# A hybrid decoder layer on one core: memory values computed by tokens, norm weights moved to ScalarE, first loads and landing estimates changed

## The chip, the cores and the metric

The kernel runs on 1 core of one Trainium2 chip. The metric is the device time of one execution in microseconds (us), median of several runs. The matmul engine is TensorE (PE in the profile; PEld is its weight load), the others are VectorE (DVE), ScalarE (ACT), GpSimd (POOL) and SyncE (SP); SP, ACT and POOL also issue DMA transfers.

## What is computed

One layer of a decoder, for 256 prompt tokens and 8 x 4 sampled tokens (288 columns in all), model width 2048, float32 throughout. Cut to what matters here:

```python
mkv = (rms_norm(mem_prompt, mem_norm_g) @ w_mem_kv).reshape(1, 256, 2, 4, 128)   # memory keys, values
h = rms_norm(x, norm_g)
c_h, c_b, c_c, c_g, q, n_g, b_g, kv6, m_q, m_g = split_cols(h @ w_in)            # 52 tiles of 128 columns
o_cmp, o_sel = nsa_cmp_sel(...)     # compressed and selected branches over a paged cache of 2048 tokens
o_win = window(...)                 # sliding window
o_m = gqa_attend(m_q, mkv keys, mkv values)                                       # memory attention
mixed = concatenate([y_conv, silu(n_g) * gated(o_cmp, o_sel, o_win), silu(m_g) * o_m])
y = rms_norm(x + mixed @ w_out, final_g)
```

The outputs are y, the new key and value rows, the window and convolution states, and the memory keys and values of the prompt (`mem_prompt_kv`).

## The kernel before

Activations lie transposed: 128 features on the partitions, tokens along the free dimension. A product of weights and activations is made in float32 precision from two parts of each operand: `wh` (the weights rounded, made by ScalarE) and `wl` (the rest, made by VectorE), and likewise `x_hl` and `m_hl`. For each 128 x 128 block three matmuls are added up: hi x hi, hi x lo, lo x hi. The weights come in **halves** `w0`, `w1`, ... of 128 x 1024 numbers, that is 8 blocks and 24 matmuls; two halves make one tile of 128 output columns. There are 152 halves: 16 of the memory weights (`w_mem`), 104 of `w_in`, 32 of `w_out`. A half is loaded into one of five buffers (`w_load`, six halves ahead), `w_hi(s + 2)` makes its `wh` two halves ahead into one of three buffers, `w_lo(s + 1)` its `wl` one half ahead into one of two. SP issues the loads up to half 13, POOL from half 14 on (`ON_SYNC`).

The order of all instructions is written by a planner in the same file, while the program is built: the main loop goes through the halves, and after every 12 matmuls `chunk()` advances a counter and lets each waiting generator (`spawn`) emit its next step. So an engine runs its instructions in exactly the order in which they were emitted, and waits where an operand is not ready. Times are guessed by a small cost table (`at[...]` for each engine); `until` and `behind` keep a generator back until an engine is thought to be done. The paged cache passes through 1024-wide staging buffers `st0` to `st5` (a seventh, in `qk1`, joins once the memory queries are used): `load_next` issues the next load as soon as a buffer is free, `loading()` estimates when it lands (`DMA_PIECE`, `DMA_LAG`), and `stage_stream` uses it when that estimate has passed. The uses are products of VectorE and GpSimd with `acmp` (`cmp_use`), scores (`sk`, `smd`) and values (`od`, `omd`) on TensorE.

The stages that the change touches, in order of time:

- Start: the first four halves multiply the memory tokens in plain float32 (`zf`), tile by tile as `memT` pieces (`mraw`, 16 planes of 128 x 256) and `w0` land; VectorE scales each piece by the norm's weights first (`mixed<-mraw`).
- Halves 4 to 15: the other six tiles of the memory weights, 256 columns wide (`proj(*m_hl, 256)`). Tiles 2 and 3 are keys. Tiles 4 to 7 are values: `mem_tile` multiplies the result by the row norm (`mvt<-z,Vc` on VectorE), a DMA writes it out, two TensorE transposes (`mvtp`) and two ScalarE copies bring it to the layout with tokens on the partitions.
- Meanwhile `prep_x` prepares x in six groups: sixteen VectorE instructions multiply by the norm's weight and the row norm (`rx<-rx,cst,rstd_x`), ScalarE and VectorE split each group into `x_hl`.
- Halves 16 to 119 (`w_in`, 288 columns), with the staged cache work and the attention of the prompt in between (`prompt_cmp`: `kcps`, `scp`, `scpt`; then `pct`, `acc`), and two passes over `w_out`.

Of the kernel before, what the change touches and what calls it, by code (L numbers as in the profile page):

```python
# [9 lines left out]
F32 = mybir.dt.float32  # L10
F32R = mybir.dt.float32r
I32 = mybir.dt.int32
AF = mybir.ActivationFunctionType
# [43 lines left out]
T_WIN = (20, 31)  # L57
T_LAST = 4
LAST_PASS = 272
DMA_PIECE, DMA_LAG = 1.75, 4.0  # L60
# [5 lines left out]
ON_SYNC = 14  # L66
# [11 lines left out]
def decode_step(ctx, tc, xT, xN, xD, memT, cst, w_in, w_mem, w_out, w_bg, pt, ptv, ckc, ckk, ckv, wk, wv, mk, mv,  # L78
                o_y, o_kv, o_mem, o_conv, o_wk, o_wv):
# [164 lines left out]
    def product_half(out, hi, lo, first, last):  # L244
        s = nhalf[0]
        nhalf[0] += 1
        w_hi(s + 2)
        w_lo(s + 1)
        wh, wl = his.pop(s), los.pop(s)
        mm = []  # L250
        for j in range(8):
            a = wh[:, j * 128:(j + 1) * 128]
            mm += [(j, a, hi(j)), (j + (0 if s > DIRECT + 1 else 4), a, lo(j)), (j + 8, wl[:, j * 128:(j + 1) * 128], hi(j))]
        mm.sort(key=lambda x: x[0])
        for n, (_, a, b) in enumerate(mm):
# [5 lines left out]
            matmul(out, a, b, start=(first and n == 0), stop=(last and n == 23))  # L261
            if n == 23 and LOW_FIRST <= s < NH - 18:
                w_lo(s + 2)
            if n % 12 == 11 and not (last and n == 23):
                chunk()
# [3 lines left out]
    def first_tiles():  # L269
# [3 lines left out]
        for k0 in (0, 8):  # L273
            for i in range(2):
# [23 lines left out]
                if k0 == 8:  # L298
                    yield z[i]

# [313 lines left out]
    def memk_use(j, t):  # L614
# [10 lines left out]
        if j == 1:  # L625
            spawn(mem_softmax(), 1)
        return
# [137 lines left out]
    rstd_m = Vc  # L765
    rstd_x = zt("C", "rstd_x")
# [23 lines left out]

    w_load(0)
# [6 lines left out]
    nc.sync.dma_start(raws[0][:, 512:], wsrc[0][:, 512:])  # L798
    m_load(4, 2, nc.scalar)
    m_load(6)  # L800
    nc.sync.dma_start(raws[1], wsrc[1])
# [68 lines left out]
    def mem_rstd():  # L870
        m_add(8)
        yield 1
        m_add(12)
        yield 1
        for n in (512, 256):
            vec.tensor_tensor(macc[:, :n], macc[:, :n], macc[:, n:2 * n], op=ALU.add)
        yield 3
        yield from token_rstd(rstd_m, [macc[:, 0:256]], 256, 1)
        env["rstd_m"] = True
        for i in range(8):  # L880
            while i not in mem_raw:
                yield 1
            dst = mem_raw[i]
            if i < 4:
                vec.tensor_tensor(dst, dst, rstd_m, op=ALU.mult)
            yield 1
            if i == 3:
                nc.gpsimd.dma_start(o_mem[0:4].rearrange("m p n -> p m n"), mkT)
            if i >= 4:
                nc.gpsimd.dma_start(o_mem[i], dst)  # L890
                yield 2
                t = ptr.tile([128, 512], F32, name=f"mvtp{i}", tag="t")
                for s in range(2):
                    transpose(t[:, s * 128:(s + 1) * 128], dst[:, s * 128:(s + 1) * 128], ident)
                for s in range(2):
                    act.activation(mvn(s, i - 4), t[:, s * 128:(s + 1) * 128], AF.Copy)
# [3 lines left out]
    def token_rstd(dst, planes, n, lag):  # L900
# [9 lines left out]
        r = small(3, "yr")  # L910
# [11 lines left out]
    def prep_x():  # L922

        g, r = C("ng"), rstd_x
# [17 lines left out]
    def sum_x():  # L942
# [25 lines left out]
        yield 2  # L968
# [39 lines left out]
    def mem_tile(i, z):  # L1008
        dst = mkT[:, i, :] if i < 4 else zt("A", "mvt")[:, :256]
        if i < 4:  # L1010
            act.activation(dst, z, AF.Copy)
        else:
            yield 2
            assert "rstd_m" in env
            vec.tensor_tensor(dst, z, rstd_m, op=ALU.mult)
        mem_raw[i] = dst
# [199 lines left out]
    def prompt_cmp():  # L1216
# [13 lines left out]
        act.activation(v, t[0:96, 128:384], AF.Copy)  # L1230
        vec.tensor_tensor(v[32:64], t[32:64, 128:384], v[32:64].bitcast(F32), op=ALU.subtract)
# [23 lines left out]
        yield 1  # L1255
        act.activation(pcv, pcv, AF.Exp, scale=SCALE)
        yield 1
        vec.tensor_reduce(sm, pcv, axis=AX.X, op=ALU.add)
# [93 lines left out]
    for i in range(2, 8):  # L1352
        then(mem_tile(i, proj(*m_hl, 256)))

# [195 lines left out]

def _inputs(x_prompt, x_sample, cache_kv, cache_win, state_conv, cache_mem, page_table, mem_prompt,
# [35 lines left out]
                w_mem=A(_ktiles(w_mem_kv[0])), w_out=A(_ktiles(wo)), w_bg=A(wbg), pt=A(pt), ptv=A(ptv), ckc=A(ckc), ckk=A(ckk), ckv=A(ckv),  # L1587
# [3 lines left out]
_OUTS = dict(o_y=(128, KT, NT), o_kv=(12, 128, NT), o_mem=(8, 128, 256), o_conv=(128, 72), o_wk=(4, 2, 128, 1024),  # L1591
# [3 lines left out]
def _outputs(r):  # L1595
# [10 lines left out]
            A(r["o_mem"].reshape(2, 4, 128, 256).transpose(3, 0, 1, 2))[None, None],  # L1606
# [16 lines left out]
```

## Time and profile before

| | us |
|---|---|
| runs | 620.51 median (618.64 to 622.23, 3 runs) |
| profiled execution, its own time | 619.23 |
| its span, first to last instruction | 616.4 |
| mean granted TensorE clock | 0.994 |
| VectorE, ScalarE, GpSimd busy | 458.6, 285.9, 200.4 |

The span is 2.8 us shorter than the execution's own time, and that execution lies 1.3 us below the median. The rows of the profile are read as engine, operation, output<-inputs, shapes, count | busy time in us, mean in ns of one | idle time of the engine before them, and what ended it.

### The profile page before, as it was taken

To read this page: it belongs to the slowest core of one execution; us is meant where nothing else is said; L and a number is where in the kernel's file an instruction comes from. 1 tells how busy PE (TensorE), PEld (TensorE's weight loads), DVE (VectorE), ACT (ScalarE), POOL (GpSimd) and SP (SyncE) were. 2 spreads that over 40 slices of the span, in tenths; PEclk is the share of its full clock that TensorE was granted. 3 is DMA by queue.
4 is the path that set the end of the run, shared out by engine and by line. 5 is a ranking of instruction groups with operands and counts; after the bars stand their busy time and mean duration, and the time that the engine had idled before them with its cause. 6 is when DMAs were issued, how large, how long until landed. Compare 5 with 4: busy or idle time off the path is not lost.

```text
span 616.4 us, 13330 instructions
## 1 busy us (share of the span) xinstructions
PE 600.2 (97%) x4893; PEld 557.9 (91%) x4893; DVE 458.6 (74%) x737; ACT 285.9 (46%) x500; POOL 200.4 (33%) x282
## 2 busy tenths in 40 slices
PE   8999999999999999999999999999999999999993
PEld 5998999989999899978998989888898898999993
DVE  5789899978477499988987879897568633357754
ACT  4855545544364345325434434353445444346650
POOL 2022545434234242323464523331212364122300
PEclk9999999999999999999999999999999999999997
DMA  8999898999888998897898998989898889677723
GB/s 313 407 403 402 261 328 314 319 312 368 310 287 303 362 388 309 295 385 267 295 316 260 318 366 288 297 283 332 303 355 321 337 285 312 225 253 276 234 86 153
DMA packets 74929, 188.40 MB, mean 306 GB/s; under 512 B 8752, under 2 KB 26064, under 8 KB 74608
## 3 DMA queue, kind: packets, MB, share of 16 engines
q0 software_dynamic: 26048, 100.48, 46.3%
q1 hardware_dynamic: 47664, 85.11, 39.0%
q10 hardware_dynamic: 1152, 1.97, 0.9%
q8 instruction: 38, 0.62, 0.4%
q14 instruction: 27, 0.22, 0.1%
HBM read 182.31 MB, written 13.60 MB: 318 GB/s over the span
## 4 chain that ended last, share of the span: by engine, by line
PE 82%; DVE 8%; DMA 6%; issue 2%; SPq 1%; ACTq 0%; ACT 0%; DVEq 0%
PE z L118 64%; PE od L118 3%; PE sk L118 3%; DMA st<-ckc 2%; PE zf L118 2%; DVE pooled L135 2%; DMA st<-ckk 2%; PE acc L118 2%; DVE wl L135 2%; PE s L118 2%; DMA qk<-ckk 1%; DMA mraw<-memT 1%; PE pt L123 1%; DVE st L135 1%; DVE ysum L135 1%
## 5 line engine op out<-in xcount | busy, mean ns | idle before, releaser
L118 PE MATMUL z<-x,wh 128*128 128x288 f32 x1664 | 254.5, 302 | 0.0
L135 DVE TENSOR_TENSOR wl<-w,wh 128x1024 fp32r<-128x1024 f32 x148 | 185.1, 1252 | 85.4 <-PE z L118 43.2
L118 PEld LDWEIGHTS z<-x,wh 128*128 128x128 f32 x1664 | 229.8, 188 | 7.8 <-issue 6.1
L135 ACT ACTIVATE wh<-w 128x1024 fp32r<-128x1024 f32 x148 | 154.4, 1052 | 19.1 <-PE z L118 14.5
L118 PE MATMUL z<-x,wl 128*128 128x288 f32 x832 | 127.0, 295 | 0.3 <-DVE wl L135 0.3
L118 PEld LDWEIGHTS z<-x,wl 128*128 128x128 f32 x832 | 115.8, 188 | 0.6 <-DVE wl L135 0.6
L350 POOL TENSOR_TENSOR st<-st,cst 128x512 f32<-128x512 f32 x63 | 69.3, 1102 | 131.5 <-DVE st L135 53.3
L219 POOL DMA_DIRECT2D w<-w_in x104 | 58.3, 560 | 109.3 <-DVE wl L135 79.2
L135 DVE TENSOR_REDUCE pooled<-st 128x16 f32<-128x1024 f32 x63 | 76.3, 1210 | 5.8 <-POOL st L350 5.8
L135 DVE TENSOR_TENSOR st<-st,cst 128x512 f32<-128x512 f32 x63 | 43.0, 684 | 10.6 <-DMA st<-ckc 10.5
L219 POOL DMA_DIRECT2D w<-w_out x32 | 17.5, 551 | 63.1 <-DVE wl L135 42.3
L578 POOL DMA_INDIRECT st<-ckv,rows_v x26 | 27.0, 1037 | 33.9 <-PE od L118 18.9
L118 PE MATMUL z<-y,wh 128*128 128x288 f32 x256 | 37.0, 297 | 0.0
L118 PE MATMUL z<-y1a,wh 128*128 128x288 f32 x224 | 35.4, 298 | 0.0
L118 PEld LDWEIGHTS z<-y,wh 128*128 128x128 f32 x256 | 35.1, 188 | 0.0
L118 PEld LDWEIGHTS z<-y1a,wh 128*128 128x128 f32 x224 | 31.4, 188 | 2.1 <-issue 1.2
L118 PE MATMUL z<-m,wh 128*128 128x256 f32 x192 | 27.3, 287 | 0.5 <-DVE mvt L135 0.5
L135 ACT ACTIVATE P<-P,nm 128x128 f32<-128x128 f32 (+1 forms) x32 | 14.2, 445 | 27.9 <-DVE nm L135 27.9
L118 PEld LDWEIGHTS z<-m,wh 128*128 128x128 f32 x192 | 24.7, 191 | 0.8 <-issue 0.7
L135 ACT ACTIVATE ysum<-z 128x288 f32<-128x288 f32 x16 | 6.6, 412 | 35.2 <-PE z L118 35.2
L118 PE MATMUL z<-y,wl 128*128 128x288 f32 x128 | 19.6, 295 | 0.0
L118 PE MATMUL sk<-st,qz 128*32 128x256 f32 x272 | 19.6, 383 | 0.0
(286 smaller groups left out, 691.6 us busy)
## 6 DMA issues: line engine op xcount, KB each, us to landing
w<-w_in POOLq DMA_DIRECT2D x104, 512.0 KB, 6.0
st<-ckc SPq DMA_DIRECT2D x126, 256.0 KB, 5.6
w<-w_out POOLq DMA_DIRECT2D x32, 512.0 KB, 5.1
st<-ckk SPq DMA_DIRECT2D x112, 128.0 KB, 4.6
w<-w_mem SPq DMA_DIRECT2D x13, 512.0 KB, 7.6
o_wk<-wk POOLq DMA_DIRECT2D x8, 512.0 KB, 6.1
o_wv<-wv POOLq DMA_DIRECT2D x8, 512.0 KB, 6.5
st<-mv SPq DMA_DIRECT2D x7, 512.0 KB, 6.5
```

Source lines behind the costliest of these rows:

```text
L118: nc.tensor.matmul(out, a, b, **kw)
L123: nc.tensor.transpose(out, a, b)
L135: return getattr(self.engine, name)(*args, **kw)
L219: (nc.gpsimd if s >= ON_SYNC else nc.sync).dma_start(raws[s], wsrc[s])
L350: done.append(eng.tensor_tensor(tm[:, :, kv], tm[:, :, kv], acmp[:, kv].unsqueeze(1).unsqueeze(1).to_broadcast([128, 2, 4, 64]), op=ALU.mu ...
L578: nc.gpsimd.indirect_dma_start(t, None, ckv, bass.IndirectOffsetOnAxis(ap=rows_v[:, j * 4 + b:j * 4 + b + 1], axis=0))
```

## The change

Five parts, in the order of the diff's weight:

1. **Memory values by tokens.** Halves 8 to 15 hold 2 blocks of 128 features by all 512 value columns (`_kpairs`). The memory tokens are now the stationary operand and the weights move: 12 matmuls of 512 columns for each half instead of 24 of 256. The result has tokens on its partitions, so ScalarE writes it with the row norm as scale (`mr`) straight to where the transposes put it; the output is written from there.
2. **Norm weights on ScalarE.** Sixteen ScalarE instructions scale x in place (`x_scales`), emitted one group for each half from half 6 on; VectorE then multiplies each group once by the row norm.
3. **First loads reordered.** Planes 4 and 5 of `memT` come from SP, planes 6 and 7 from ACT; the second part of `w0` and `w1` are cut in two.
4. **Estimates.** `DMA_LAG` 4.0 becomes 7.5 and, from chunk 165 on, 6.0; `DMA_PIECE` 1.75 becomes 1.6. Staging starts at chunk 22 (`STAGE_AT`), SP issues the loads up to half 18, the window's copies start later (`T_WIN`). Two waits between VectorE and ScalarE in `prompt_cmp` are counted (`behind`, `until`).
5. **An eighth staging buffer:** `qmz`, once the memory scores have used it.

```diff
-T_WIN = (20, 31)
+T_WIN = (33, 30)
-DMA_PIECE, DMA_LAG = 1.75, 4.0
+DMA_PIECE, DMA_LAG, LATER = 1.6, (7.5, 6.0), 165
+STAGE_AT = 22
-ON_SYNC = 14
+ON_SYNC = 19
...
-        return max(at[1], at[SYNC]) + DMA_LAG
+        return max(at[1], at[SYNC]) + DMA_LAG[now[0] >= LATER]
...
+    def run_half(s, mm, last, between=None):
+        m = len(mm) // 2
+        for n, (out, a, b, start, stop) in enumerate(mm):
...
-            if n == LOAD_AT:
+            if n == LOAD_AT * m // 12:
                 w_load(s + WR + 1)
                 next(x_next, None)
+                if s > 5:
+                    next(x_scale, None)
...
+    def mem_values():
+        z = [pz.tile([128, 512], F32, name=f"zv{tt}", tag="z") for tt in range(2)]
+        def out(tt):
+            planes = mixed[:, 12 + 2 * tt:14 + 2 * tt, 0:256]
+            act.activation(planes, z[tt].rearrange("p (a n) -> p a n", a=2), AF.Copy, scale=mr[:, tt:tt + 1])
+            nc.gpsimd.dma_start(o_memv[tt].rearrange("p (a n) -> p a n", a=2), planes)
+        for h in range(8):
...
+            for tt in range(2):
+                for k in range(2):
+                    hi, lo = (m_hl[n][:, 2 * h + k, tt * 128:(tt + 1) * 128] for n in range(2))
+                    w = slice(k * 512, (k + 1) * 512)
...
+                    mm += [(early, tt, hi, wh[:, w]), (early, tt, lo, wh[:, w]), (2.5 if h == 7 and not tt else 4, tt, hi, wl[:, w])]
...
         if j == 1:
             spawn(mem_softmax(), 1)
+            free.append(qmz.rearrange("p c b h n -> p (c b h n)"))
+            load_next()
...
+    def x_scales():
+        for i in range(6):
+            yield
+            k, t = xg[i]
+            for j in range(t.shape[1] // NT):
+                act.activation(xr[k + j], xr[k + j], AF.Copy, scale=C("ng")[:, k + j:k + j + 1])
...
-    nc.sync.dma_start(raws[0][:, 512:], wsrc[0][:, 512:])
-    m_load(4, 2, nc.scalar)
-    m_load(6)
-    nc.sync.dma_start(raws[1], wsrc[1])
+    m_load(4, 2)
+    nc.scalar.dma_start(raws[0][:, 512:768], wsrc[0][:, 512:768])
+    nc.sync.dma_start(raws[0][:, 768:], wsrc[0][:, 768:])
+    m_load(6, 2, nc.scalar)
+    for i in range(0, 1024, 512):
+        nc.sync.dma_start(raws[1][:, i:i + 512], wsrc[1][:, i:i + 512])
...
-                for j in range(k, k + n):
-                    vec.scalar_tensor_tensor(xr[j], xr[j], g[:, j:j + 1], r, op0=ALU.mult, op1=ALU.mult)
+                xv = x.rearrange("p (k n) -> p k n", n=NT)
+                vec.tensor_tensor(xv, xv, r.unsqueeze(1).to_broadcast([128, n, NT]), op=ALU.mult)
...
-        yield 1
+        yield from until(VEC, AHEAD)
+        behind(ACT, VEC)
         act.activation(pcv, pcv, AF.Exp, scale=SCALE)
         yield 1
+        behind(VEC, ACT)
         vec.tensor_reduce(sm, pcv, axis=AX.X, op=ALU.add)
...
-    for i in range(2, 8):
+    for i in range(2, 4):
         then(mem_tile(i, proj(*m_hl, 256)))
+    mem_values()
```

How the order moves, at the three places that the prediction leans on. First TensorE at half 8, the first of the values: before, 24 matmuls of 256 columns into `z` for each half; here the end of half 8 and the beginning of half 9.

```order
L118 MATMUL z_422<-m_110,wh_325 128x256
L118 MATMUL z_422<-m_111,wh_325 128x256
L118 MATMUL z_422<-m_110,wl_386 128x256 x8
L118 MATMUL z_422<-m_110,wh_384 128x256
L118 MATMUL z_422<-m_111,wh_384 128x256
```

After, the same place: 12 matmuls of 512 columns for each half, `zv` for the two groups of 128 tokens.

```order
L119 MATMUL ssq<-cst,mr 128x128 x2
L119 MATMUL zv_428<-wh_328,m_110 128x512
L119 MATMUL zv_428<-wh_328,m_111 128x512
L119 MATMUL zv_427<-wl_388,m_110 128x512 x2
L119 MATMUL zv_428<-wl_388,m_110 128x512 x2
L119 MATMUL zv_427<-wh_386,m_110 128x512
L119 MATMUL zv_427<-wh_386,m_111 128x512
```

The four `mvtp` pairs of transposes, which stood inside halves 12, 14, 16 and 18, are gone.

Second, ScalarE while the values are computed, before (each `wh` is one half of the weights, `x` a group's rounded part).

```order
L135 ACTIVATE wh_384<-w_257 128x1024
L135 ACTIVATE mixed<-z_324 128x256
L135 ACTIVATE rstd_x<-rx 128x288
L135 ACTIVATE wh_423<-w_281 128x1024
L135 ACTIVATE Vc<-ssq 128x256
L135 ACTIVATE x_112<-rx_247 128x864
L135 ACTIVATE wh_465<-w_316 128x1024
L135 ACTIVATE x_112<-rx 128x864
L135 ACTIVATE wh_512<-w_355 128x1024
```

And after, the same stretch with the groups' scaling.

```order
L136 ACTIVATE wh_386<-w_260 128x1024
L136 ACTIVATE rx_250<-rx_250,cst 128x288 x3
L136 ACTIVATE mixed<-z_327 128x256
L136 ACTIVATE rstd_x<-rx 128x288
L136 ACTIVATE wh_429<-w_284 128x1024
L136 ACTIVATE Vc<-ssq 128x256
L136 ACTIVATE rx<-rx,cst 128x288 x3
L136 ACTIVATE x_112<-rx_250 128x864
L136 ACTIVATE wh_460<-w_319 128x1024
L136 ACTIVATE x_112<-rx 128x864
L136 ACTIVATE rx<-rx,cst 128x288 x3
L136 ACTIVATE wh_486<-w_358 128x1024
```

Each group's three scalings now stand ahead of a `wh`, from half 10's on.

Third, SP's first loads, before, with what they wait for (DMAHW0 to DMAHW7 are the eight semaphores that the loads of SP and ACT take in turn).

```order
L798 DMA w_118<-w_mem 128x512
L770 DMA mraw_114<-memT 128x512
L801 DMA w_119<-w_mem 128x1024 [waits DMAHW0_49]
L770 DMA mraw_115<-memT 128x512 [waits DMAHW1_49]
L770 DMA mraw_115<-memT 128x512 [waits DMAHW2_49]
```

After:

```order
L815 DMA mraw_114<-memT 128x512
L854 DMA w_119<-w_mem 128x256
L857 DMA w_120<-w_mem 128x512 [waits DMAHW1_49]
L857 DMA w_120<-w_mem 128x512 [waits DMAHW2_49]
L815 DMA mraw_115<-memT 128x512 [waits DMAHW3_49]
L815 DMA mraw_115<-memT 128x512 [waits DMAHW4_49]
```

The ninth load, the first that waits for an earlier one to land, was `w1` on SP; it is now planes 6 and 7 of `memT` on ACT, and `w1` follows in two pieces.

More of the change, by code (lines that the diff above doesn't have):

```diff
@@ L254, in product_half @@
         mm.sort(key=lambda x: x[0])
-        for n, (_, a, b) in enumerate(mm):
+        run_half(s, [(out, a, b, first and n == 0, last and n == 23) for n, (_, a, b) in enumerate(mm)], last)
+    def run_half(s, mm, last, between=None):
+        m = len(mm) // 2
+        for n, (out, a, b, start, stop) in enumerate(mm):
             if s == DIRECT and n == 0:
                 w_load(s + WR)
-            if n == LOAD_AT:
+            if n == LOAD_AT * m // 12:
                 w_load(s + WR + 1)
                 next(x_next, None)
-            matmul(out, a, b, start=(first and n == 0), stop=(last and n == 23))
-            if n == 23 and LOW_FIRST <= s < NH - 18:
+                if s > 5:
+                    next(x_scale, None)
+            matmul(out, a, b, start=start, stop=stop)
+            if n == 2 * m - 1 and LOW_FIRST <= s < NH - 18:
                 w_lo(s + 2)
-            if n % 12 == 11 and not (last and n == 23):
+            if n == 7 and between:
+                between()
+            if n == m - 1:
+                chunk()
+            if n == 2 * m - 1 and not last:
                 chunk()
@@ L299, in first_tiles @@
                     yield z[i]
+    def mem_values():
[5 more added lines that the diff above has]
+        for h in range(8):
+            s = nhalf[0]
+            nhalf[0] += 1
+            w_hi(s + 2)
+            w_lo(s + 1)
+            wh, wl = his.pop(s), los.pop(s)
+            mm = []
+            for tt in range(2):
+                for k in range(2):
+                    hi, lo = (m_hl[n][:, 2 * h + k, tt * 128:(tt + 1) * 128] for n in range(2))
+                    w = slice(k * 512, (k + 1) * 512)
+                    early = 2 * tt + (k if h == 7 and tt else 0)
+                    mm += [(early, tt, hi, wh[:, w]), (early, tt, lo, wh[:, w]), (2.5 if h == 7 and not tt else 4, tt, hi, wl[:, w])]
+            mm.sort(key=lambda x: x[0])
+            i = [[n for n, x in enumerate(mm) if x[1] == tt] for tt in range(2)]
+            run_half(s, [(z[tt], a, b, h == 0 and n == i[tt][0], h == 7 and n == i[tt][-1]) for n, (_, tt, a, b) in enumerate(mm)],
+                     h == 7, (lambda: out(0)) if h == 7 else None)
+        assert "rstd_m" in env
+        out(1)
+        chunk()
     def proj(hi, lo, N):
@@ L765, in decode_step @@
     rstd_m = Vc
+    mr = one.tile([128, 2], F32, name="mr")
     rstd_x = zt("C", "rstd_x")
@@ L877, in mem_rstd, with token_rstd @@
         yield 3
-        yield from token_rstd(rstd_m, [macc[:, 0:256]], 256, 1)
+        yield from token_rstd(rstd_m, [macc[:, 0:256]], 256, 1, mr)
         env["rstd_m"] = True
-        for i in range(8):
+        for i in range(4):
             while i not in mem_raw:
                 yield 1
-            dst = mem_raw[i]
-            if i < 4:
-                vec.tensor_tensor(dst, dst, rstd_m, op=ALU.mult)
+            vec.tensor_tensor(mem_raw[i], mem_raw[i], rstd_m, op=ALU.mult)
             yield 1
[L887 to L896, printed above, removed]
+        nc.gpsimd.dma_start(o_mem.rearrange("m p n -> p m n"), mkT)
     GROUPS = ((0, 0), (128, 0), (160, 96))
-    def token_rstd(dst, planes, n, lag):
+    def token_rstd(dst, planes, n, lag, r):
         groups = [x for x in GROUPS if x[0] + 128 <= n]
@@ L967, in sum_x @@
         nc.sync.dma_start(wbg, w_bg)
-        yield 2
+        while now[0] < STAGE_AT:
+            yield 1
         for t in buffers:
@@ L1008, in mem_tile @@
     def mem_tile(i, z):
[L1009 to L1016, printed above, removed]
+        act.activation(mkT[:, i, :], z, AF.Copy)
+        mem_raw[i] = mkT[:, i, :]
+        return
+        yield
     cos, sin = C("cos"), C("sin")
@@ L1254, in prompt_cmp @@
         vec.tensor_tensor(pcv, pcv, bc(mx), op=ALU.subtract)
-        yield 1
+        yield from until(VEC, AHEAD)
+        behind(ACT, VEC)
         act.activation(pcv, pcv, AF.Exp, scale=SCALE)
         yield 1
+        behind(VEC, ACT)
         vec.tensor_reduce(sm, pcv, axis=AX.X, op=ALU.add)
```

14 lines of the change are left out of this document (8 added, 6 removed).

## The prediction

> **What bounds the kernel now.** I read the page first, then TensorE's waits, then the windows of the early stage.
>
> ```profile
> span 616.4 us, 13330 instructions
> PE 600.2 (97%) x4893; PEld 557.9 (91%) x4893; DVE 458.6 (74%) x737; ACT 285.9 (46%) x500; POOL 200.4 (33%) x282
> PE 82%; DVE 8%; DMA 6%; issue 2%; SPq 1%; ACTq 0%; ACT 0%; DVEq 0%
> ```
>
> TensorE is busy for 97% of the span and carries 82% of the chain that ended last. A busy row alone could hide stalls, so the second view is what TensorE waited for in all.
>
> ```profile
> PE zf L118 <- DVE mixed L135: 1.8, 3, 0.9
> PE pct L123 <- DVE pc L135: 1.2, 1, 1.2
> PE sk L118 <- DMA qk<-ckk: 0.7, 1, 0.7
> PE z L118 <- DVE mvt L135: 0.5, 1, 0.5
> ```
>
> Columns: total us, times, longest. These four come to 4.2 us; nothing else is over 1.1. So the kernel is a queue of matmuls. A change gains what it takes out of that queue plus what it removes of these few waits, and loses the waits that it makes. The other engines have little room in one place, where x is prepared:
>
> ```profile
> 40.00:50.00 10.00, 10.00 (x86) 10.00 (x85) 10.00 (x18) 5.42 (x7) 3.46 (x6) 1.00 1.03 397
> 50.00:60.00 10.00, 9.49 (x89) 8.73 (x91) 10.00 (x15) 5.68 (x10) 3.22 (x6) 1.00 1.04 404
> ```
>
> After the window's length stand the busy times of PE, PEld, DVE, ACT, POOL, then clock, DMA share and GB/s. VectorE is full there, ScalarE half busy, the DMA engines full at 400 GB/s.
>
> **Values by tokens: matmuls.** A half of 24 matmuls of 256 columns, then two ScalarE rows that repeat with each half of 24 matmuls of 288 columns late in the kernel:
>
> ```profile
> 37.45 2.08 PE L118 MATMUL z<-m,wh 128*128 128x256 f32 x16
> 40.33 2.08 PE L118 MATMUL z<-m,wh 128*128 128x256 f32 x16
> 564.35 0.45 ACT L135 ACTIVATE ysq<-ysum 128x288 f32<-128x288 f32 x1 [1.23 <-DVE ysum L135]
> 567.55 0.45 ACT L135 ACTIVATE ysq<-ysum 128x288 f32<-128x288 f32 x1 [1.24 <-DVE ysum L135]
> ```
>
> From start to start 2.88 / 24 = 0.120 us and 3.20 / 24 = 0.1333 us: 32 columns cost 0.0133 us, 0.000417 for a column. At 512 columns the line gives 0.120 + 256 x 0.000417 = 0.2267. Eight halves cost 192 x 0.120 = 23.04 us now and 96 x 0.2267 = 21.76 after: **-1.3**. No row has a stream of 512-wide matmuls of this kind; the nearest are isolated ones:
>
> ```profile
> L118 PE MATMUL z<-m,wh 128*128 128x256 f32 x192 | 27.3, 287 | 0.5 <-DVE mvt L135 0.5
> L118 PE MATMUL acc<-pcT,vcp 96*128 96x512 f32 x4 | 1.7, 425 | 0.3 <-DVE pcT L135 0.3
> ```
>
> One of 512 columns lasts 138 ns longer than one of 256, so the step is at most 0.120 + 0.138 = 0.258, together 24.8 us (+1.7). From below, 512 columns can't go faster than the 288 of the row above, 0.1333: 12.8 us (-10.2). I take the line through two streams.
>
> The Trainium skill, page "TensorE: Matmul & The Clock Gate", section "Back-to-back issue gap", has for a real stream of weight loads and matmuls about 131 ns each at 512 columns. By that figure, an estimate, the eight halves would last 12.6 us and the change gain 10.5 there. Against it: the trace needs 133 ns for 288 columns already, and the four lone ones last 425 ns against 287.
>
> **Values by tokens: what stood between.** The transposes and the wait for `mvt`:
>
> ```profile
> 46.09 1.60 PE L118 MATMUL z<-m,wh 128*128 128x256 f32 x12
> 47.53 0.38 PE L123 MATMUL mvtp<-cst,mvt 128*128 128x128 f32 x2
> 49.19 2.08 PE L118 MATMUL z<-m,wh 128*128 128x256 f32 x16
> 52.77 1.67 PE L118 MATMUL z<-m,wh 128*128 128x256 f32 x12 [0.51 <-DVE mvt L135]
> ```
>
> The half from 46.09 to 49.19 holds a pair of transposes and lasts 3.10, that is 0.22 over 2.88; four pairs make **-0.9**. The next, to 52.77, lasts 3.58: 0.70 of waiting for `mvt`, which had to empty `z` before the tile after next: **-0.7**. What is late there next is the same `z` buffer, emptied by one ScalarE copy for each token group, only twice. In all **-2.9** for this part, which no other engine covers, since TensorE never stops behind it.
>
> **Norm weights on ScalarE.** The prices:
>
> ```profile
> L135 ACT ACTIVATE ysum<-ysum,cst 128x288 f32<-128x288 f32 x16 | 8.6, 537 | 0.6
> 571.23 0.54 ACT L135 ACTIVATE ysum<-ysum,cst 128x288 f32<-128x288 f32 x1
> 571.67 1.05 ACT L135 ACTIVATE wh<-w 128x1024 fp32r<-128x1024 f32 x1
> L135 ACT ACTIVATE x<-rx 128x864 fp32r<-128x864 f32 x5 | 4.6, 928 | 7.9 <-DVE rx L135 5.8 <-DMA rx<-xT 2.1
> L135 DVE SCALAR_TENSOR_TENSOR rx<-rx,cst,rstd_x 128x288 f32<-128x288 f32 x16 | 7.3, 505 | 0.0
> L135 DVE TENSOR_TENSOR mvt<-z,Vc 128x256 f32<-128x256 f32 x4 | 1.6, 410 | 0.0
> L135 DVE TENSOR_TENSOR ysum<-ysum,rb 128x864 f32<-128x864 f32 x3 | 3.0, 1045 | 0.0
> ```
>
> A scaling is the same as `ysum<-ysum,cst`: 0.537 alone, 0.44 until the next starts. Sixteen put 7.0 us on ScalarE. VectorE loses 7.3 + 1.6 and gets 5 x 1.045 + 0.46 (one of 288 columns) = 5.7: 3.2 us less in its full stretch. That relief is worth nothing by itself, as TensorE waits for VectorE there only at `mvt`. The danger is ScalarE. For a half it now runs 1.05 (`wh`) + 0.93 (`x`) + 3 x 0.44 = 3.3 us, and the half lasts 12 x 0.2267 = 2.7. Five such halves lose 2.9 us, and the first group, ahead of half 10's `wh`, 1.3: 4.2 of its lead. How long is the lead?
>
> ```profile
> 34.47 1.05 ACT L135 ACTIVATE wh<-w 128x1024 fp32r<-128x1024 f32 x1
> ```
>
> This is half 10's `wh`, done at 35.52; TensorE begins half 10 at 40.33: 4.8 us. So about 0.6 is left, and each group also passes from ScalarE to VectorE and back. A scaling also waits for its group of x to land, with a `wh` behind it on ScalarE; the casts wait for that now, 2.1 us in all. I charge **+0.4**, between 0 and 2.5 (the 0.537 in full adds 1.6, the hand-overs the rest).
>
> The Trainium skill, page "ScalarE: Activation LUTs", section "Rules for kernel authors", says to put multiplications on VectorE, not ScalarE. By it this part would lose; per instruction the rows agree (0.537 against 0.505), but here VectorE is the full engine.
>
> **First loads.**
>
> ```profile
> 2.14 0.43 SPq L770 DMA_DIRECT2D mraw<-memT  x1
> 4.18 0.33 SPq L801 DMA_DIRECT2D w<-w_mem  x1
> 2.17 6.12 DMA mraw<-memT
> 6.88 1.13 PE L118 MATMUL zf<-mixed,w 128*128 128x256 f32 x4 [0.86 <-DVE mixed L135]
> 8.72 12.35 PE L118 MATMUL zf<-mixed,w 128*128 128x256 f32 x56 [0.71 <-DVE mixed L135]
> ```
>
> A plain float32 matmul of a plane costs 12.35 / 28 = 0.44. Planes 2 and 3 start at 6.88 and end at 7.75; planes 4 and 5, which land at 2.17 + 6.12 = 8.29, start at 8.72. They now go ahead of 512 KB, some 1.2 us at 400 GB/s, so that wait of 0.97 goes. What is late next are planes 6 and 7: they are now the load that waits for the first one to land and is issued at about 4.2, not 2.1. With the same bytes ahead they land at 8.3 to 8.9, and TensorE takes them at 8.7 to 9.3 instead of 8.72 + 2 x 0.44 = 9.6. **-0.4**, between -0.9 and +0.5.
>
> **Estimates, staging buffer, counted waits.** In the order, 12 matmuls stand between `kcps` and `scp` now, and 64 after; between `scpt` and `pct` 64 and 82. So the 1.2 us at `pct` should go, and a later use gives the load behind the `sk` wait time to land (0.7). That is 1.9; for waits that take their place, which no row shows, I give half of it back: **-1.0**, between -2.8 (all of the waits behind the start) and +6 (the rival below). The eighth buffer and the loads moved from POOL to SP cost no engine time on TensorE's path; SP's queue then holds halves 14 to 18 ahead of the staging loads, which are used only after half 16.
>
> **Sum:** -2.9 + 0.4 - 0.4 - 1.0 = **-3.9**. From the profiled execution's own 619.23 that is 615.3, from the median of the runs, 620.51, it is 616.6; I forecast their middle, **616.0**, and give the rivals' times from the same middle, 619.9.
>
> **Rivals.**
>
> *ScalarE takes over.* If the groups' hand-overs use up the lead, TensorE waits for `wh` or `wl` from half 12 to 15: the term is +2.5, the sum -1.8 (-2.9 + 2.5 - 0.4 - 1.0), 618. For it: a lead of 0.6. Against it: 46% busy overall, and VectorE's 3.2 us of relief. Chance 0.18.
>
> *The waits only move.* Start and mid-kernel keep their waits; -2.9 + 0.4 = -2.5, 617.4. This is also the case in which the first loads don't do what they say, since their ninth still waits. Chance 0.17.
>
> *Late landings stop VectorE: slower.* Uses run on VectorE in order, ahead of the next `wl`.
>
> ```profile
> 254.74 14.87 DMA st<-ckc
> st<-ckc SPq DMA_DIRECT2D x126, 256.0 KB, 5.6
> ```
>
> A load that usually lands in 5.6 us took 14.87 where memory keys and cache came together. Met by its use, it stops VectorE for 9.3 us; `wl` is one half (3.2) ahead, so TensorE loses 6.1. With eight buffers more loads are in flight at once. One such meeting makes -3.9 + 6.1 = +2.2, 622; two make it slower, +8.3, 628. Against it: landings are assumed 2 to 3.5 us later than now. It decides from the second meeting on. Chance of two 0.09, of one 0.06.
>
> *512 columns stream like 288.* -10.2 in place of -1.3: 607. Chance 0.02.
>
> The forecast (614 to 617.3) has 0.48.
>
> **How the numbers follow.** A measurement of this kernel can tell about 0.5%, 3.1 us, from no change, so faster means below 617.4 against the median. The forecast lies on the near side by 1.4, so about 0.44 of its 0.48 fall there, as do 0.04 of ScalarE's case, 0.08 of the moved waits' and 0.02 of the fast stream: 0.58. Slower: 0.09, and 0.01 of the single meeting: 0.10. Same: 0.32. The range 612 to 621 leaves out the fast stream and the two meetings and holds the unknown costs' ends down to -8.
>
> **What the new profile would show.** `zv` halves 2.7 us apart (2.9 or more: the matmul term is wrong). The values end now where `bg` begins:
>
> ```profile
> 58.90 2.15 PE L118 MATMUL bg<-rx,qmz 128*32 128x288 f32 x32
> ```
>
> They should end near 56.3 (58.9 less 1.3, 0.7 and two of the four transposes, 0.4, with 0.2 for the start). Waits of TensorE for ScalarE or VectorE between 45 and 57 would show the first rival. `zf` in one run from about 7 us on would show the first loads right. No `pct` wait over 0.5 us, and no wait of VectorE for a staging load above 3 us with a TensorE gap behind it. The forecast falls if TensorE's busy time doesn't drop by 2.5 to 3.5 us.

## The result, and the profile after

| | before | after |
|---|---|---|
| runs, median us | 619.45 (617.17 to 624.27, 16 runs) | 622.30 (621.96 to 626.49, 16 runs) |
| ratio to before, 95% interval | | 1.0064 [1.0042, 1.0085] |
| profiled execution, own time / span | 619.23 / 616.4 | 621.99 / 620.2 |

The change makes the kernel slower by 0.64%; 616.0 had been forecast, with 621 as the upper end. Since the runs of before scatter by 7 us, the ratio and its interval count, not one run.

The page after: span, busy times, the shares of the chain that ended last, and two groups in which VectorE works on the staging buffers.

```profile
span 620.2 us, 13128 instructions
PE 600.7 (97%) x4789; PEld 551.5 (89%) x4789; DVE 455.1 (73%) x723; ACT 293.3 (47%) x510; POOL 201.1 (32%) x275
PE 81%; DVE 11%; issue 4%; POOL 1%; ACT 1%; DMA 1%; DVEq 0%; POOLq 0%; ACTq 0%
...
L136 DVE TENSOR_TENSOR st<-st,cst 128x512 f32<-128x512 f32 x58 | 42.2, 731 | 0.8 <-DMA st<-ckc 0.8
```

DMA has all but left the chain (6% to 1%), and VectorE has more of it (8% to 11%). The last row is the one to read against before's:

```profile
L135 DVE TENSOR_TENSOR st<-st,cst 128x512 f32<-128x512 f32 x63 | 43.0, 684 | 10.6 <-DMA st<-ckc 10.5
```

VectorE had waited 10.5 us for landings and now waits 0.8: the new estimates do what they say. But TensorE had felt little of those 10.5 us: behind the start, all its waits for VectorE came to 2.6 us in before. The largest, 1.2 at `pct`, did stand behind two such landings: VectorE had waited 0.76 and 1.64 us for them between 266 and 270 us, just ahead of `pct`'s operand. What TensorE waits for, after (total us, times, longest):

```profile
PE acc L119 <- DVE pcT L136: 1.7, 2, 0.9
PE ot L124 <- DVE odr L136: 1.1, 1, 1.1
PE zf L119 <- DVE mixed L136: 0.9, 3, 0.4
PE otm L124 <- DVE odr L136: 0.9, 1, 0.9
PE z L119 <- DVE wl L136: 0.9, 1, 0.9
PE sm L119 <- ACT S L136: 0.8, 1, 0.8
PE ptmd L124 <- ACT qk L136: 0.4, 1, 0.4
PE sc L119 <- ACT S L136: 0.4, 1, 0.4
PE pe L124 <- DVE smc L136: 0.4, 1, 0.4
```

The waits for `pct`, `sk` and `mvt` are gone as forecast (1.2, 0.7 and 0.5), and nine of 0.4 us or more stand where there were four (not counting the start's `zeros`, 1.1 in both).

Where the time went is read from three places in TensorE's rows. The stream of the values and its end (the first `z<-x`), and the second pass over `w_out` (the first `z<-y,wh`), first of after, then of before:

```profile
45.33 1.98 PE L119 MATMUL zv<-wh,m 128*128 128x512 f32 x8
48.05 1.98 PE L119 MATMUL zv<-wh,m 128*128 128x512 f32 x8
56.76 1.84 PE L119 MATMUL z<-x,wh 128*128 128x288 f32 x12
554.62 1.62 PE L119 MATMUL z<-y,wh 128*128 128x288 f32 x11
```

```profile
550.84 1.35 PE L118 MATMUL z<-y,wh 128*128 128x288 f32 x9
```

The values end at 56.76 in place of 58.90: 2.1 us ahead. At the second pass the kernel is 3.8 us behind. So 5.9 us are lost in between, where the change has taken work from TensorE (two pairs of transposes) and added none. One of the new waits from near, VectorE's rows and then TensorE's:

```profile
370.43 1.22 DVE L136 TENSOR_TENSOR wl<-w,wh 128x1024 fp32r<-128x1024 f32 x1
371.57 0.69 DVE L136 TENSOR_TENSOR st<-st,cst 128x512 f32<-128x512 f32 x1
372.17 0.34 DVE L136 TENSOR_SCALAR odr<-od,cst 128x128 f32<-128x128 f32 x1
372.55 0.35 DVE L136 SCALAR_TENSOR_TENSOR odr<-od,cst,odr 128x128 f32<-128x128 f32 x1
...
373.05 0.30 PE L124 MATMUL ot<-cst,odr 128*128 128x128 f32 x1 [1.10 <-DVE odr L136]
```

Two instructions of 0.35 us stand behind a weights' subtraction and a staged product; the transpose `ot`, placed one chunk after them, comes 1.1 us too early. Most of the new waits are of this kind, for a small step of a softmax or an output on VectorE: of TensorE's 7.5 us of waits between the values' end and the second pass, 5.2 are for VectorE and 2.3 for ScalarE; none of 0.2 us or more is for a DMA.

### The profile page after: what moved, and what is told of

It reads as the page before. It is cut to its first block, busy times and chain, and to the rows that moved or that the text cites. A ratio compares the mean times of both kernels' runs of the same rounds, so it can differ in the third digit from the quotient of the medians.

```text
span 620.2 us, 13128 instructions
## 1 busy us (share of the span) xinstructions
PE 600.7 (97%) x4789; PEld 551.5 (89%) x4789; DVE 455.1 (73%) x723; ACT 293.3 (47%) x510; POOL 201.1 (32%) x275
## 4 chain that ended last, share of the span: by engine, by line
PE 81%; DVE 11%; issue 4%; POOL 1%; ACT 1%; DMA 1%; DVEq 0%; POOLq 0%; ACTq 0%
PE z L119 61%; PE zv L119 4%; PE sk L119 3%; PE od L119 3%; DVE wl L136 2%; DVE pooled L136 2%; PE zf L119 2%; PE acc L119 2%; PE s L119 1%; DMA mraw<-memT 1%; DVE st L136 1%; DVE ysum L136 1%; PE pt L124 1%; PE pv L124 1%; DVE mx L136 1%
## 5 line engine op out<-in xcount | busy, mean ns | idle before, releaser
L392 POOL TENSOR_TENSOR st<-st,cst 128x512 f32<-128x512 f32 x58 | 65.2, 1126 | 117.5 <-DVE st L136 54.1
L136 DVE TENSOR_REDUCE pooled<-st 128x16 f32<-128x1024 f32 x58 | 70.1, 1209 | 3.4 <-POOL st L392 3.4
L136 ACT ACTIVATE se<-z 128x288 f32<-128x288 f32 x16 | 6.5, 409 | 32.2 <-PE z L119 32.2
L119 PE MATMUL z<-y1a,wl 128*128 128x288 f32 x128 | 19.5, 294 | 0.0
```

What stands on the lines that cost most here:

```text
L119: nc.tensor.matmul(out, a, b, **kw)
L136: return getattr(self.engine, name)(*args, **kw)
L392: done.append(eng.tensor_tensor(tm[:, :, kv], tm[:, :, kv], acmp[:, kv].unsqueeze(1).unsqueeze(1).to_broadcast([128, 2, 4, 64]), op=ALU.mu ...
```

## The experiments

Two theories. **O**: whatever shifts the planner's clock deals the order behind 60 us anew, and the new order is worse; the work itself has become cheaper. **S**: a part of the change itself (its scaling, its place, its estimates, its buffer) makes the waits. All times are medians; "before" is the kernel before in the same session. The sessions' medians of before lie between 617.56 and 619.45, so runs of different sessions are compared by their ratios.

| run | what | us | before | ratio, 95% interval |
|---|---|---|---|---|
| e1 | after, estimates, eighth buffer and counts undone | 623.83 | 618.50 | 1.0062 [1.0034, 1.0090] |
| e2 | after, estimates undone | 622.48 | 618.50 | 1.0057 [1.0035, 1.0078] |
| e3 | after, eighth buffer undone | 627.83 | 618.50 | 1.0142 [1.0089, 1.0195] |
| e4 | after, counts undone | 623.11 | 618.50 | 1.0071 [1.0039, 1.0104] |
| e5 | part 1 alone | 619.74 | 618.65 | 1.0005 [0.9973, 1.0037] |
| e6 | part 1, order of before | 618.97 | 618.65 | 0.9996 [0.9956, 1.0036] |
| e7 | parts 1 and 2, order of before | 618.92 | 618.65 | 1.0008 [0.9969, 1.0048] |
| e8 | after without part 1, order of after | 624.75 | 618.65 | 1.0078 [1.0048, 1.0109] |
| e9 | e6, the `sk` use near 209 us later | 616.56 | 617.56 | 0.9971 [0.9942, 0.9999] |
| e10 | before, that use later | 617.92 | 617.56 | 1.0014 [0.9979, 1.0049] |
| e11 | before, `CMP_GAP` 1.80 | 622.34 | 617.56 | 1.0062 [1.0028, 1.0096] |
| e12 | before, cost of a matmul +1 ns | 617.55 | 617.56 | 1.0004 [0.9979, 1.0028] |
| e13 | order of after, five steps later (leaves two heads ungated) | 628.83 | 617.78 | 1.0171 [1.0148, 1.0195] |
| e14 | e9 and part 2 | 614.99 | 617.78 | 0.9965 [0.9944, 0.9985] |
| e15 | e14 and part 3 | 615.46 | 617.78 | 0.9964 [0.9944, 0.9984] |
| e16 | order of after, steps later off the chain | 620.82 | 618.68 | 1.0032 [1.0011, 1.0054] |
| e17 | estimates, eighth buffer and counts alone | 625.76 | 618.68 | 1.0100 [1.0061, 1.0140] |

**Undoing one part of after at a time (e1 to e4).**

```diff
# e2; e1 also has the edits of e3 and e4
-DMA_PIECE, DMA_LAG, LATER = 1.6, (7.5, 6.0), 165
+DMA_PIECE, DMA_LAG, LATER = 1.75, (4.0, 4.0), 165
# e3
-            free.append(qmz.rearrange("p c b h n -> p (c b h n)"))
-            load_next()
# e4
-        behind(VEC, ACT)
         vec.tensor_tensor(v[32:64], t[32:64, 128:384], v[32:64].bitcast(F32), op=ALU.subtract)
...
-        yield from until(VEC, AHEAD)
-        behind(ACT, VEC)
+        yield 1
         act.activation(pcv, pcv, AF.Exp, scale=SCALE)
         yield 1
-        behind(VEC, ACT)
```

> The changed kernel with the landing estimates of before (1.75 a piece, lag 4.0 throughout), without the eighth buffer and without the counted waits; values by tokens, the scaling on ScalarE and the new first loads stay. The trace of after shows the values ending some 2 us ahead and 5.9 us of new waits of TensorE after 60 us. Theory E (the estimates, buffer and counts make the waits): those 5.9 us go, 615.5 to 617. Theory O (the planner's order behind 60 us is dealt anew by whatever shifts it, and its waits come out at random): anywhere between 615 and 622, with other waits than before's. Theory S (the scaling on ScalarE or the values' place makes the waits): 620 to 623, as after.

> The changed kernel with only the landing estimates taken back (1.75 a piece, 4.0 for every load). If the later lag (7.5 and 6.0) is what pushes the uses of the staged tiles on top of the softmax work on VectorE: 616 to 617.5, and the waits of TensorE for pcT, odr and wl between 250 and 375 us go. If the eighth buffer or the counts are the cause: 621 to 623. If the order is only dealt anew: anything from 616 to 623 with new places of the waits.

> The changed kernel without the eighth staging buffer. If the eighth buffer is the cause (more uses ready at a time): 616 to 618. If the estimates are: 621 to 623 (unchanged). If the order is dealt anew: 616 to 623 with new places.

> The changed kernel without the two counted dependencies (behind and until in prompt_cmp and vcp). They moved the waits at pct (1.4 us before) to acc behind pcT. If they are the cause: 617 to 619. If not: 621 to 623, and the wait at pct is back at about 1.2 us.

None wins the time back (e1 and e3 lie above every range that was expected), and each has its waits elsewhere. In e1, which has neither estimates nor buffer nor counts, one wait is the largest:

```profile
PE otm L124 <- DVE odr L136: 2.8, 1, 2.8
```

In e2 the two largest are `pt` behind `P` (1.9) and `otm` (1.1). No single removal wins it back, so the theory that the estimates push the uses onto the softmax work fell as it stood. What all have in common is a new order. All four also keep the later start of the staging, the loads on SP up to half 18 and the later window copies (`STAGE_AT`, `ON_SYNC`, `T_WIN`); no run takes those alone out of after, so what they add to the loss isn't known. The `pct` wait did not return in e4 either (0.2).

**Pinning the order (e5 to e8).** To keep the order apart from the work, e6 to e8 have the planner's clocks at every chunk and the chunk of every staged use written in from another kernel. In e6, behind the values, all five engines then run in exactly the order of before, but for the transposes and multiplies that are gone, with their copies and outputs.

```diff
         now[0] += 1
+        if now[0] in PLAN:
+            at[:] = PLAN[now[0]]
         for item in list(live):
...
-            while (now[0] < due - EARLY or needs.get(u) not in env or len(tiles_of.get((u, j), ())) < pieces(u) or at[0] < ready[u, j]
-                   or u is cmp_use and (at[0] < last_cmp + CMP_GAP or at[VEC] > at[0] + BACKLOG)):
+            while now[0] < USE_AT[i] or needs.get(u) not in env or len(tiles_of.get((u, j), ())) < pieces(u):
```

> The kernel before with the memory values by tokens alone (scaling, first loads, estimates, buffers and counts as before), the planner left to set the order behind them. Theory O (the values shift the planner's clock, it deals the order of uses and softmax steps anew behind 60 us, and the new order holds more waits of TensorE): 617 to 623, with TensorE's excess over its cadence 2 to 8 us above before's. Theory S (something else than the order, such as the scaling, makes the waits): 616 to 617.5 here, 2 us under before.

> The same kernel as e5 with the planner's clocks at each chunk and the chunk of each use written in from the kernel before: behind the values every engine has its instructions in the order of before, but for eight transposes and four multiplies of the values that are gone. Theory O: 616 to 617.5, 2 to 2.5 us under before (its median here 618.5 to 619.5), the waits behind 60 us those of before. If the values by tokens themselves bring the waits (their copies on ScalarE, where their result lies): 619 to 623, with the waits for odr and S that after has.

> As e6, and the scaling by the norm weights on ScalarE as well. Theory O: as e6 within 0.7 us, 616 to 618, since the scaling adds 16 instructions to ScalarE before 60 us only. Theory S: 619 to 623 with waits of TensorE behind 60 us that e6 lacks.

> The changed kernel with the values by features as before, but with the order of the changed kernel written in (clocks and uses by chunk). Theory O: the waits behind 60 us are those of after (pcT, odr, wl, S), and the values cost what they did before: 623 to 626. If the waits came of the values by tokens and not of the order: 618 to 621.

The traces separate order and work at once. e8 has before's values, but after's order; its waits (first five but for the start) are after's, row for row:

```profile
PE acc L426 <- DVE pcT L443: 1.7, 2, 0.9
...
PE ot L431 <- DVE odr L443: 1.1, 1, 1.1
PE otm L431 <- DVE odr L443: 0.9, 1, 0.9
PE z L426 <- DVE wl L443: 0.9, 1, 0.9
PE sm L426 <- ACT S L443: 0.8, 1, 0.8
```

By the ratios it costs 0.9 us more than after (1.0078 and 1.0064), with intervals that overlap. So the order brings the waits, whichever way the values are made; what the values by tokens save is read from the stage itself, further down. e6 has the values by tokens and before's order, and none of these waits; its profiled span is 613.5, 2.9 under before's. But its median lies at before's, where 2 us less were expected, and so does e7's. The scatter is one reason: e6's ten runs lie between 614.7 and 622.6, e7's between 615.6 and 624.3, while after's lie between 622 and 626.5. The order of before has a weak place that shows in only some executions. e7's profile caught it:

```profile
PE sk L426 <- DMA qk<-ckk: 4.2, 1, 4.2
```

It is the meeting that cost 0.7 in the trace of before: the scores of the fourth batch of selected keys, near 209 us, reach TensorE about when the last pages land.

**That use later, and small deals of the order (e9 to e12).** e9 and e10 move that use by two chunks (one half), and with it the two staged uses that queue behind it; e11 and e12 change one number of the planner's in the kernel before.

```diff
# e9, e10: the entry with number 36 of the list of uses
-USE_AT[36] = 113
+USE_AT[36] = 115
# e11
-CMP_GAP = 1.75
+CMP_GAP = 1.8
# e12
-        k, t = ((0, n / 2400 + 0.0115) if b.dtype == F32R else (1, n * 0.00048 + 0.008) if out.shape[0] == 32
+        k, t = ((0, n / 2400 + 0.0125) if b.dtype == F32R else (1, n * 0.00048 + 0.008) if out.shape[0] == 32
```

> As e6 (values by tokens, order of before), with one use moved: the scores of the fourth batch of selected keys (sk, near 209 us) come one half later. In the trace of before TensorE reached that use 0.7 us ahead of the last page's landing, in e7 4.2 us. Theory L (the runs of before's order differ by how late those pages land): the spread narrows to about 2 us, median 614.5 to 616.5, some 2 to 4 under before. If the spread has another source: median 617 to 619 as e6, and the spread stays at 8 us.

> The kernel before with that use one half later and nothing else. Theory L: median 616 to 617.5 with a spread of about 2 us, 1.5 to 2 above e9 (the price of the values by features). If the spread has another source: as before, 618 to 619.5.

> The kernel before with one number of the planner moved by 3 percent (the least gap of two uses of compressed pages 1.80 for 1.75). No work changes; the order behind 270 us is dealt anew. Theory O (any new deal costs, because the order of before had few waits by luck or by search): 619 to 623. If the waits of after come of its own numbers: 618 to 619.5 as before.

> The kernel before with the planner's cost of a matmul 1 ns higher (0.0125 for 0.0115); no work changes, the order behind 190 us is dealt anew. Theory O: 618 to 623, with waits of TensorE at other places. Otherwise 618 to 619.5.

e9 comes out faster than before, if barely (the interval ends at 0.9999), and its twelve runs lie within 2.6 us (615.0 to 617.6). e10's median, 617.92, is before's (1.0014) and above the 616 to 617.5 of theory L, and its spread has not narrowed: five of its twelve runs still lie between 619 and 625.1. So the late pages can be one source of the scatter, as e7 and e9 suggest, but not the only one. The granted clock shows where to look for the rest: four of these five runs are e10's only ones with a mean granted clock under 0.994, and of the 125 runs of before in the sessions, the 34 with such a clock have a median of 620.9 us, the others 617.8. What lowers the clock is taken up in the last section. e11 and e12 move no work. A gap of 1.80 for 1.75 costs 0.62%, as much as the whole change; one nanosecond on a matmul costs nothing, where theory O had expected at least 618. Of the waits of e11:

```profile
PE sk L118 <- DMA st<-ckk: 2.2, 2, 1.7
...
PE z L118 <- ACT y1a L135: 1.3, 1, 1.3
```

Of the nine orders that the planner dealt anew (after, e1 to e5, e11, e12, e17) seven are slower than before beyond their intervals, two the same, none faster.

**After's waits taken away (e13, e16).** Both have after's order written in. e13 lets five steps wait one chunk more, among them `acc`, which lies on the prompt's chain; e16 leaves that chain's length and issues `acc` behind its batch's first scores. In e13 the last batch of the prompt's attention is written only after two of its heads have been gated, so that these heads' outputs go into the last product ungated for those tokens.

```diff
# e13 and e16, ahead of pe, ot, otm (and of ptmd, behind until(ACT))
         yield from until(VEC)
+        yield 1
         t = ptr.tile([128, 512], F32, name=f"ot{hf}", tag="t")
# e13
         yield from until(VEC)
+        yield 1
         matmul(acc, vcp[:, g, :], own, start=True, stop=False, skip_group_check=True)
# e16: the same line moved behind the scores s of br 1
+            if br == 1:
+                matmul(acc, vcp[:, g, :], own, start=True, stop=False, skip_group_check=True)
             vec.tensor_reduce(mx, P, axis=AX.X, op=ALU.max)
```

> The changed kernel, its clocks and uses by chunk written in, and five steps that TensorE waited at in the trace of after (acc behind pcT, ot and otm behind odr, pe, ptmd) one chunk, some 1.6 us, later. If those waits are the loss (1.06 + 0.92 + 1.26 + 1.03 + 0.74 + 0.60 of the gaps over 0.3 us, 5.6 us in all): 617 to 619, 4 to 5 under after. If VectorE as a whole is short there, the waits move on: 621 to 623.

> The changed kernel, its clocks and uses by chunk written in; ot, otm, pe and ptmd one chunk later, and the product acc behind pcT issued after its batch's first scores, so that the prompt's chain keeps its length. If the waits at these five are the loss: their 5.6 us of gaps go and the time falls by 3 to 5 us, 617.5 to 619.5. If they only show a lack of VectorE: 621 to 623.

In e13 the five waits are gone and others are there; at 628.83 it lies above both ranges expected:

```profile
PE sk L426 <- DMA st<-wk: 3.1, 1, 3.1
PE z L426 <- ACT y1a L443: 2.6, 1, 2.6
PE z L426 <- DVE wl L443: 1.9, 2, 1.0
```

The prompt's chain has grown by four chunks, and TensorE arrives at the first pass over `w_out` before its operand `y1a` is split. Each of the two longest waits is also followed by 3.4 us at half the clock. e16 avoids that and gains 1.5 us on after by the medians, 2.0 by the ratios (1.0032 and 1.0064, with intervals that overlap). Some of the rest has moved to the weights:

```profile
PE z L426 <- DVE wl L443: 1.8, 3, 0.9
...
PE z L426 <- ACT wh L443: 0.9, 3, 0.4
```

So the waits themselves are likely a part of the loss, and VectorE is short of time in those stretches as well; neither end of the expectation holds alone.

**The parts at one order (e14, e15), and the planner's part alone (e17).** The edits of e14 and e15 are those of parts 2 and 3 in the change, with e9's order; e17 is the kernel before with the following lines of the change (not `STAGE_AT`, `ON_SYNC` and `T_WIN`).

```diff
-DMA_PIECE, DMA_LAG = 1.75, 4.0
+DMA_PIECE, DMA_LAG, LATER = 1.6, (7.5, 6.0), 165
...
+            free.append(qmz.rearrange("p c b h n -> p (c b h n)"))
+            load_next()
...
+        behind(VEC, ACT)
         vec.tensor_tensor(v[32:64], t[32:64, 128:384], v[32:64].bitcast(F32), op=ALU.subtract)
...
-        yield 1
+        yield from until(VEC, AHEAD)
+        behind(ACT, VEC)
         act.activation(pcv, pcv, AF.Exp, scale=SCALE)
         yield 1
+        behind(VEC, ACT)
```

> e9 with the scaling by the norm weights on ScalarE, the order otherwise that of e9. My prediction charged the scaling 0.4 us (0 to 2.5): 616.5 to 617.2 against e9's 616.6. If the copies of ScalarE stand in the way of the weights at 40 to 57 us: 618 to 619. If VectorE's relief counts: 615.5 to 616.3.

> e14 with the first loads reordered as in the change (the weights' first tile in more pieces and on another queue, the staging's start as before). My prediction: 0.4 us less than e14 (from 0.5 more to 0.9 less). If the first loads decide nothing: within 0.5 of e14.

> The kernel before with the fourth part of the change alone: landing estimates 7.5 and 6.0, 1.6 a piece, the eighth staging buffer, the two counted dependencies. My prediction credited this part with 1.0 us (from 2.8 less to 6 more): 616 to 618. Theory O: a new deal of the order, 618 to 623, but with no wait of sk for a landing and a spread under 3 us.

e17 is slower by 1.0%, more than either range allowed, with the same kind of waits:

```profile
PE pt L123 <- DVE P L135: 1.7, 1, 1.7
PE otm L123 <- DVE odr L135: 1.7, 1, 1.7
PE pe L123 <- DVE odr L135: 1.6, 1, 1.6
PE od L118 <- DMA st<-ckv,rows_v: 1.3, 1, 1.3
```

e14 and e15 are the fastest kernels of the study, though their intervals overlap e9's. What the scaling does is seen between 40 and 58 us, e9 first, then e14 (window, its length, then PE, PEld, DVE, ACT, POOL, clock, DMA share, GB/s), with e9's wait there:

```profile
PE zv L426 <- DVE wl L443: 0.7, 2, 0.4
40.00:58.00 18.00, 17.30 (x75) 13.20 (x73) 18.00 (x28) 11.53 (x13) 3.96 (x7) 1.00 1.03 397
```

```profile
40.00:58.00 18.00, 17.97 (x78) 14.31 (x78) 17.67 (x20) 16.19 (x24) 4.51 (x8) 1.00 1.04 401
```

In e9 VectorE is busy for all 18.00 us, and TensorE waits for `wl`; in e14 that wait is gone and TensorE is busy for 17.97 of 18 us. How long the eight halves of the values take, from their first matmul to the first one behind them, in e9 and then in e14:

```profile
35.41 0.73 PE L426 MATMUL zv<-wh,m 128*128 128x512 f32 x2
59.55 0.45 PE L426 MATMUL bg<-rx,qmz 128*32 128x288 f32 x4
35.57 0.73 PE L426 MATMUL zv<-wh,m 128*128 128x512 f32 x2
58.58 0.45 PE L426 MATMUL bg<-rx,qmz 128*32 128x288 f32 x4
```

That is 24.14 us without the scaling and 23.01 with it. The same stretch lasts 24.84 in before (34.06 to 58.90), 24.15 in e6, 22.99 in e15 and 22.93 in after, and in e8, which has the values by features with the scaling and the rest of the change, 23.99. These differences lie far outside the 0.1 us by which kernels with the same work here differ. From e15's page (its span is 613.4 us):

```profile
PE 600.2 (98%) x4789; PEld 552.5 (90%) x4789; DVE 455.7 (74%) x723; ACT 292.5 (48%) x510; POOL 201.0 (33%) x280
```

## Why the prediction was wrong

**Values by tokens, -2.9: the matmul's price was right, the part's own gain was not.** The `zv` halves are 48.05 - 45.33 = 2.72 us apart, 0.2267 for a matmul of 512 columns, just the line through the two streams. The rival that they stream like 288 columns, and with it the figure of 131 ns that the Trainium skill, page "TensorE: Matmul & The Clock Gate", section "Back-to-back issue gap", has for 512 columns, doesn't hold for these matmuls. The values end 2.1 us earlier where 2.6 were promised. But "which no other engine covers" failed: with this part alone (e6, e9) the eight halves take 24.15 us for before's 24.84, so only 0.7 us comes of it, because TensorE then waits for `wl`. The rest came only together with the scaling.

**Norm weights on ScalarE, +0.4: the sign was wrong.** In the stage that it touches the scaling gains 1.1 us (24.14 to 23.01), and 0.85 even with the old values (24.84 to 23.99, e8), and no wait for ScalarE arises there. The whole times don't show it: e14 and e9 differ by 0.4 us in its favour by their ratios, e7 and e6 by 0.7 against it, all within the intervals. The sentence that failed is "that relief is worth nothing by itself, as TensorE waits for VectorE there only at `mvt`". When the values get faster, `wl` is late next, 0.7 us in e6 and e9, and the relief of VectorE removes it. I had asked what is late next behind `z` only. Both parts together take 1.8 us out of the eight halves and, with the two pairs of transposes that stood later, some 2.3 in all, where -2.5 was summed; so that sum came out near by two errors that cancel.

**First loads, -0.4: not to be seen.** e15 and e14 differ by less than their scatter. With and without the new first loads, the plain products end anywhere between 20.2 and 22.2 us in the traces; the four traces above 22 (e7, e8, e9, e14) all had 3.4 us of half clock from about 7.5 us on, and no other had. In after `zf` still starts in three runs, with 0.9 us of waits for 1.8, where one run from 7 us was promised.

**Estimates, buffer, counts, -1.0: this step failed.** I credited the waits at `pct` and `sk` (1.9) and wrote "for waits that take their place, which no row shows, I give half of it back". The credited waits went, but alone the estimates, the buffer and the counts cost 1.0% (e17), 6 to 7 us. The credit itself was read from one execution: with the same order around it, TensorE's wait at `pct` is 1.2 us in before, 0.8 in e14, 0.4 in e10 and none in e6, e7, e9 and e15, and the one at `sk` is 0.7 in before, 4.2 in e7 and none in e6. The upper bound of +6 was there, but tied to one mechanism, late landings that stop VectorE, and these became fewer: 10.5 us of waiting for `ckc` fell to 0.8. The loss came from the order that goes with the estimates. Between the values' end and the second pass TensorE's waits in the view come to 7.5 us in after against 2.8 before, which is 4.7 of the 5.9 us. The granted clock is no part of it (0.994 and 0.995 in the mean, no stretch at half clock behind the start in either trace but at the very end). Where the other 1.2 lies stays open.

**What lay under all steps:** I counted a new order only for the estimates, the buffer and the counts. e1 has none of these and is as slow as after; e5 has part 1 alone and keeps nothing of the gain. The change moves the planner's clock by some 2 us (at chunk 60, in the clocks written into e6 and e8, 104.6 and 102.3), and in e5 the faster halves alone were enough for a new order. Where the old order, with the one use moved, meets the cheaper work (e14, e15), 0.36% is gained on before, 2.2 us of the 2.9 that the first three terms said. The rivals missed it too: "the waits only move" had the kind, but assumed the old waits stay and priced no new ones.

**Of the marks** that I had set, TensorE's busy time was of no use: it is 600.2 in before and in e15, whose span is 3.0 us shorter. It counts the modelled ends of overlapping matmuls; the idle remainder and the waits are what moved.

**Open:** which property makes an order good. The runs show that before's order is at the good end of ten, not why. Which of the estimates, the buffer and the counts costs most can't be told either, since each removal deals the order again, and `STAGE_AT`, `ON_SYNC` and `T_WIN` were never tried alone.

## What to carry to other kernels

Where a planner with a cost table sets the order, a change of a few us in one stage re-deals all that follows, and the new order can cost more than the change saves: measure a part first with the old order pinned. Waits of a helper engine for transfers are worth removing only as far as the bottleneck engine waits behind them: here 9.7 us of VectorE's waiting went, and TensorE had felt some 1.2 of it; e15 still has 8.3 us of such waiting and is among the fastest. A wait of a microsecond in one trace should be looked for in a second execution before it is credited. And a relief of a full engine has to be priced in the stage as it will be after the other parts, not as it is.

## What the runs showed of the hardware

**A stop of TensorE can cost more than itself, and its length alone doesn't tell when.** e7 from its wait of 4.2 us on (window, length, PE, PEld, DVE, ACT, POOL, granted clock, DMA share, GB/s), then e11 behind its wait of 1.7 us, and e1 behind its wait of 2.8:

```profile
212.00:215.00 3.00, 0.27 (x4) 0.23 (x8) 0.00 (x0) 0.00 (x0) 0.00 (x0) 0.60 0.96 364
215.00:218.00 3.00, 3.00 (x32) 2.20 (x25) 1.04 (x3) 0.91 (x3) 1.26 (x2) 0.50 1.05 409
218.00:221.00 3.00, 3.00 (x20) 3.00 (x20) 0.82 (x1) 1.55 (x5) 0.92 (x2) 0.77 1.04 409
```

```profile
160.00:163.30 3.30, 3.30 (x17) 1.72 (x17) 0.00 (x0) 0.60 (x1) 0.00 (x0) 0.50 0.88 288
```

```profile
487.00:490.00 3.00, 2.90 (x20) 2.63 (x21) 0.90 (x5) 1.91 (x5) 2.08 (x4) 1.00 0.96 326
```

In e7 the granted clock is 0.50 from 212.6 to 219.4 us, 4.7 us of it after work has resumed; from 215 to 221 that loses 3 x 0.5 + 3 x 0.23 = 2.2 us beside the wait. In the clock records of all traces a stretch at 0.50 inside the kernel lasts 3.41 or 6.83 us. That it is slower is seen in the matmuls: in e13, behind its stop of 2.6 us, eight of 288 columns take 1.90 us where before has 1.22.

```profile
498.26 1.90 PE L426 MATMUL z<-y1a,wl 128*128 128x288 f32 x8
549.79 1.22 PE L118 MATMUL z<-y1a,wl 128*128 128x288 f32 x8
```

Behind the first 20 us, stops of 1.7 (e11), 2.6 and 3.1 (e13), 3.3 (e3) and 4.2 us (e7) were followed by such a stretch; those of 1.6 to 1.7 in e17 and of 2.8 in e1 were not. The Trainium skill, page "TensorE: Matmul & The Clock Gate", section "What's actually happening", has the slow state follow at least one idle window of about 3.4 us, in windows that run free of the kernel. The length of the stretches agrees with such a window; the stops of e11 and e13 that were enough are shorter, and there the measurement decides. What else decides is open. By these figures (half of 3.41 us) a late landing can cost 1.7 us or more on top of its wait in one execution and nothing in the next, which fits the scatter of before's runs by their clock; in which stretch those runs lost it isn't known.

**VectorE and GpSimd hold each other up.** In after's timeline, a staged product of VectorE with GpSimd idle, and then one beside GpSimd's:

```profile
265.46 0.68 DVE L136 TENSOR_TENSOR st<-st,cst 128x512 f32<-128x512 f32 x1
266.28 1.95 POOL L392 TENSOR_TENSOR st<-st,cst 128x512 f32<-128x512 f32 x1 [3.10 <-DMA qk<-mk]
267.20 1.58 DVE L136 TENSOR_TENSOR st<-st,cst 128x512 f32<-128x512 f32 x1
```

Over the whole trace of after, the 26 subtractions `wl` that overlap one of GpSimd's products take 1424 ns in the mean, the other 122 take 1221. Eighteen of the 26 are within 60 ns of those; eight take 1.36 to 2.65 us. The Trainium skill, page "SBUF — State Buffer", section "Who interferes with whom", says that a VectorE instruction with two inputs in SBUF contends with a GpSimd instruction that reads SBUF; the rows agree. The planner's cost table prices an instruction of VectorE by its size alone, so an order that lays more of them side by side is dearer than it is planned. Here that is small: before has 21 such meetings (1445 ns in the mean), five fewer, about 1 us of VectorE's time by these means.
